# Decays' sums in one pass, reordered stage ends and a shared start in a nine-stage float32 network

## The chip, the cores and the metric

The kernel runs on one NeuronCore of a Trainium2 chip. The metric is the device time of one execution in microseconds; the time of a kernel is the median of its runs. Lines of the profile (L170) are lines of the kernel before. Its engines are called PE (TensorE's matmuls), PEld (its weight loads), DVE (VectorE), ACT (ScalarE), POOL (GpSimd) and SP (SyncE, which issues most transfers).

## The reference

256 tokens of width 1024, all in float32. A first block of two layers; each layer has a gated feed-forward network (hidden width 2816), a mixer, a cross attention to 256 memory tokens and a second feed-forward network, each between a norm before and a norm behind. Then a second block (a state-space branch and a dilated attention branch, mixed, then a third kind of feed-forward network) and a last norm. The change touches the start, the feed-forward networks' beginnings, the mixer and the norms. In the mixer half of the heads are a gated delta rule in both directions:

```
g = -exp(a_log) * softplus(a + dt_bias)          # per token, direction and head
g = cumsum(g)                                     # in each chunk
decay = exp(where(tril, g[i] - g[j], -inf))
lower = strict_lower((k*beta) @ k.T * decay)
sol   = triangular_solve(I + lower, [v*beta, k*beta*exp(g)])
qk    = (q @ k.T) * decay
...                                               # state from chunk to chunk
rms_norm(x, w) = x * rsqrt(mean(x*x) + 1e-6) * w
x = x + 0.5 * rms_norm(swiglu(rms_norm(x, pre)), post)
```

## The kernel before

Tokens are two tiles of 128 partitions. Each weight matrix comes in units of 128x1024 numbers (512 KB) through four raw buffers, on SP's queue; ACT rounds a unit to a high part (L148) and DVE subtracts for the low part (L149), in halves of 512 columns. Activations are split the same way behind a transposition (to_xT, L250; split, L175 and L177). Each product is then three matmuls, high by high, high by low, low by high (L170 to L172). An instruction stream per engine runs in its own order; a list scheduler sets that order from a model of times, except where issue_after holds an instruction behind another on its engine. The stages run one after the other: ffn1, mix, xat, ffn2, twice, then the second block and its ffn.

The start: sixteen matmuls of zeros (L1791), x of tile 0, the first norm's gain broadcast to 128 partitions, two units, x of tile 1, two units. set_pre multiplies x by the gain (L235) and take_pre transposes and splits it. In a feed-forward stage norms are deferred: the products are made from x times gain, and the norm's factor (rstd, computed by small operations, L189 to L193, after sums of squares on ACT, L205) comes in with the tanh (L364) and the products that follow (L365, L366). The first two blocks of 256 hidden columns are made by tokens (by_tokens: first tile 0 for both blocks, then tile 1, since tile 1's residual is still under way from the stage before: run_late); h is transposed (L371) and split. The other nine blocks are made by channels.

A stage ends with residual for each tile: the factor from the sums of squares on POOL (rstd with gpsimd), the product with the norm's gain (L296, L298), the update of x (L300), and set_pre for the next stage, with a second factor on POOL when the norm isn't deferred (L237).

In the mixer, strengths makes g, the prefix sums by a product with a triangle (L764), and decays(d) for a direction: for each of four heads, three times, a product whose stationary operand is one column of g, broadcast, and whose moving operand is the triangle (L805), so that all partitions hold the prefix sums as a row; masks are added by a product with the identity (L807); twelve exponentials on ACT follow. f32 products leave two records each in the trace; fp32r products one. In solve, four heads of two directions are solved with matmuls of 64 partitions and 64 columns in opposite quarters of the array (L1145, L1153), six phases a mixer. All this goes on beside fill, a stream of projections of which more(1) issues one step.

Rotary tables for the retention heads are made during the first feed-forward stage by its hook, which takes one step of a generator after each block by channels.

## Time and profile before

| what | value |
|---|---|
| median of 3 runs | 1946.12 us (1944.95 to 1948.43) |
| the profiled execution | 1947.42 us |
| its span, first to last instruction | 1945.2 us |
| mean granted TensorE clock | 0.998 |
| busy: PE, PEld, DVE, ACT, POOL | 1914.7, 1717.7, 1412.7, 1048.9, 185.7 us |
| matmul records | 12859 |
| read from HBM | 333.90 MB, 172 GB/s over the span |

The busy time of PE counts modelled ends of pipelined matmuls: what one matmul costs is read from the start of one to the start of the next. A row of the timeline may merge several instructions (x8).

### The profile page before, as it was taken

To read this page: it belongs to the slowest core of one execution; us is meant where nothing else is said; L and a number is where in the kernel's file an instruction comes from. 1 tells how busy PE (TensorE), PEld (TensorE's weight loads), DVE (VectorE), ACT (ScalarE), POOL (GpSimd) and SP (SyncE) were. 2 spreads that over 40 slices of the span, in tenths; PEclk is the share of its full clock that TensorE was granted. 3 is DMA by queue.
4 is the path that set the end of the run, shared out by engine and by line. 5 is a ranking of instruction groups with operands and counts; after the bars stand their busy time and mean duration, and the time that the engine had idled before them with its cause. 6 is when DMAs were issued, how large, how long until landed. Compare 5 with 4: busy or idle time off the path is not lost.

```text
span 1945.2 us, 34675 instructions
## 1 busy us (share of the span) xinstructions
PE 1914.7 (98%) x12859; PEld 1717.7 (88%) x12859; DVE 1412.7 (73%) x3002; ACT 1048.9 (54%) x2173; POOL 185.7 (10%) x407
## 2 busy tenths in 40 slices
PE   9999999999999999999999999999999999999998
PEld 6899888898899989999788978998999998888997
DVE  6777688775666766667987757666798988767765
ACT  5655465465554555546555645554555555546542
POOL 2000100020200110010100120002101111001000
PEclk9999999999999999999999999999999999999999
DMA  8666434364566556644434726655566646656651
GB/s 266 206 220 217 125 109 147 109 220 137 164 205 196 180 186 220 187 161 144 137 101 145 247 86 212 200 189 157 146 174 182 187 121 205 200 196 224 199 179 49
DMA packets 272887, 337.26 MB, mean 173 GB/s; under 512 B 19740, under 2 KB 223150, under 8 KB 272718
## 3 DMA queue, kind: packets, MB, share of 16 engines
q1 hardware_dynamic: 266980, 326.64, 53.6%
q10 hardware_dynamic: 5690, 8.25, 1.2%
q8 instruction: 101, 1.65, 0.3%
q14 instruction: 68, 0.56, 0.1%
q0 software_dynamic: 48, 0.16, 0.0%
HBM read 333.90 MB, written 1.08 MB: 172 GB/s over the span
## 4 chain that ended last, share of the span: by engine, by line
PE 84%; DVE 4%; POOL 3%; DMA 2%; ACT 2%; issue 2%; SPq 0%; ACTq 0%; POOLq 0%; DVEq 0%
PE bank L170 25%; PE bank L171 25%; PE bank L172 25%; DVE lo L149 2%; DMA raw<-in_ffn_up_dram 2%; PE bank L250 1%; POOL t L192 1%; POOL vh L213 1%; POOL y L193 1%; ACT hi L148 1%; PE bank L1003 1%; PE bank L1543 1%; ACT md L1034 1%; PE bank L1153 1%; PE bank L1256 1%
## 5 line engine op out<-in xcount | busy, mean ns | idle before, releaser
L148 ACT ACTIVATE hi<-raw 128x512 fp32r<-128x512 f32 (+1 forms) x1190 | 678.7, 615 | 413.6 <-PE bank L172 96.0
L149 DVE TENSOR_TENSOR lo<-raw,hi 128x512 fp32r<-128x512 f32 (+1 forms) x1190 | 764.7, 680 | 187.1 <-ACT hi L148 178.4
L170 PE MATMUL bank<-xh,hi 128*128 128x256 f32 x2080 | 588.8, 283 | 0.0
L171 PE MATMUL bank<-xl,hi 128*128 128x256 f32 x2080 | 585.1, 281 | 0.0
L172 PE MATMUL bank<-xh,lo 128*128 128x256 f32 x2080 | 584.7, 281 | 0.1
L170 PEld LDWEIGHTS bank<-xh,hi 128*128 128x128 f32 x2080 | 394.2, 190 | 4.1
L171 PEld LDWEIGHTS bank<-xl,hi 128*128 128x128 f32 x2080 | 393.9, 189 | 3.5
L172 PEld LDWEIGHTS bank<-xh,lo 128*128 128x128 f32 x2080 | 394.5, 190 | 0.6 <-DVE lo L149 0.6
L170 PE MATMUL bank<-hi,xh 128*128 128x512 f32 (+1 forms) x852 | 333.5, 392 | 3.5 <-ACT xh L175 2.2
L171 PE MATMUL bank<-lo,xh 128*128 128x512 f32 (+1 forms) x852 | 324.7, 381 | 5.2 <-DVE lo L149 5.1
L172 PE MATMUL bank<-hi,xl 128*128 128x512 f32 (+1 forms) x852 | 323.9, 380 | 0.5 <-DVE xl L177 0.5
L171 PEld LDWEIGHTS bank<-lo,xh 128*128 128x128 f32 x852 | 160.3, 188 | 34.8 <-DVE lo L149 9.9
L170 PEld LDWEIGHTS bank<-hi,xh 128*128 128x128 f32 x852 | 160.2, 188 | 31.5 <-ACT xh L175 3.5
L172 PEld LDWEIGHTS bank<-hi,xl 128*128 128x128 f32 x852 | 159.9, 188 | 28.8 <-DVE xl L177 2.2
L170 PE MATMUL bank<-hi,hh 128*128 128x512 f32 x440 | 175.9, 400 | 1.3 <-ACT hh L175 1.3
L171 PE MATMUL bank<-lo,hh 128*128 128x512 f32 x440 | 173.9, 395 | 0.0
L172 PE MATMUL bank<-hi,hl 128*128 128x512 f32 x440 | 173.4, 394 | 0.0
L213 POOL TENSOR_SCALAR vh<-ss 128x1 f32<-128x1 f32 x40 | 27.6, 689 | 1130.8 <-ACT junk L205 996.1
L402 ACT ACTIVATE th<-s 128x256 f32<-128x256 f32 x90 | 37.3, 414 | 124.3 <-DVE s L401 122.7
L172 PEld LDWEIGHTS bank<-hi,hl 128*128 128x128 f32 x440 | 82.7, 188 | 20.7 <-DVE hl L177 0.3
L170 PEld LDWEIGHTS bank<-hi,hh 128*128 128x128 f32 x440 | 82.7, 188 | 18.4 <-ACT hh L175 1.7
L171 PEld LDWEIGHTS bank<-lo,hh 128*128 128x128 f32 x440 | 82.7, 188 | 16.0
(369 smaller groups left out, 1991.4 us busy)
## 6 DMA issues: line engine op xcount, KB each, us to landing
raw<-in_w_in_dram SPq DMA_DIRECT2D x112, 512.0 KB, 4.4
raw<-in_ffn_gate_dram SPq DMA_DIRECT2D x176, 256.0 KB, 3.9
raw<-in_ffn_up_dram SPq DMA_DIRECT2D x176, 256.0 KB, 4.3
raw<-in_ffn_down_dram SPq DMA_DIRECT2D x88, 512.0 KB, 4.6
raw<-in_w_in_dram SPq DMA_DIRECT2D x96, 192.0 KB, 2.8
raw<-in_w_ffn_gate_dram SPq DMA_DIRECT2D x44, 256.0 KB, 3.8
raw<-in_w_ffn_up_dram SPq DMA_DIRECT2D x44, 256.0 KB, 4.1
raw<-in_w_ffn_down_dram SPq DMA_DIRECT2D x22, 512.0 KB, 4.6
```

Source lines behind the costliest of these rows:

```text
L148: nc.scalar.activation(hi[:, c], raw[:, c], AF.Copy)
L149: nc.vector.tensor_tensor(lo[:, c], raw[:, c], hi[:, c].bitcast(F32), ALU.subtract)
L170: mm(out, lhsT=lh, rhs=rh, start=start, stop=False)
L171: mm(out, lhsT=lh, rhs=rl, start=False, stop=False)
L172: mm(out, lhsT=ll, rhs=rh, start=False, stop=stop)
L192: V.tensor_scalar(t, y, y, vh, ALU.mult, ALU.mult)
L193: V.tensor_scalar(y, t, -1.5, y, ALU.add, ALU.mult)
L213: V.tensor_scalar(vh, s[:, 0:1], s[:, 1:2], 0.5 * EPS, ALU.add, ALU.add)
L250: self.nc.tensor.transpose(b[:, i * P:(i + 1) * P], src[:, (q + i) * P:(q + i + 1) * P], self.ident)
L402: last["A"] = nc.scalar.activation(th, s[:, 0], AF.Tanh)
L1003: T.matmul(b[:, j * 256:(j + 1) * 256], lhsT=lhs[:, h, j * P:(j + 1) * P], rhs=rhs[:, h], start=True, stop=True)
L1034: A.activation(md[r, :, :, :, s], mn[r, :, :, c0:c0 + 16].rearrange("p n h a -> p a h n"), AF.Copy, scale=self.half[s][r])
```

## The change

1. Decays: the prefix sums of each direction and tile are made once, as rows, on 36 partitions (32 to 35 repeat 0 to 3): g is copied to two places of a zeroed tile, four f32 products with the triangle make the rows, ACT rounds all 36 to fp32r, and DVE puts the residue on partitions 32 to 35. Then, for each head, one fp32r product with a 0/1 column (selr, broadcast) lays the sums of both directions and both tiles on all partitions, with both masks added, and a second one gives the unmasked far sums. decays is called with two heads for both directions in place of one direction for four heads. The chunk's total, once read off a row's end, is now a product with ones.
2. Solve: the matmuls of one phase are held in the order of (head, direction), each behind the one before.
3. Stage ends: residual's factor, and set_pre's when the norm isn't deferred, are computed on DVE; POOL keeps the deferred ones. In a feed-forward stage the update of x of tile 1 and its set_pre are held behind the tanh and the last product of the first block by tokens (self.behind).
4. First stage alone: the first two blocks by tokens alternate between the tiles after every two contraction steps, so that one unit serves both.
5. Start: the gain comes as eight rows of 128 and is transposed; x is transposed without it, and each 128-column split multiplies by its column. Unit 0 is loaded before tile 1 of x; twelve warm-up matmuls in place of sixteen.
6. Rotary tables for both tiles at once, with one sine, behind an added step of the generator.
7. Weight pools in the feed-forward stages by a fixed rule; the raw pool lies at the other side of the memory.

```
-        self.rawp = pool(ctx, "raw", 4)
+        self.rawp = ctx.enter_context(tc.tile_pool(name="raw", bufs=4, side="right", reuse_waits="tile"))
...
+            for i in range(m):
+                ix = (slice(None), k0 + q + i, slice(t * P, (t + 1) * P))
+                self.split(xT[0][ix], xT[1][ix], b[:, i * P:(i + 1) * P], cols[:, q + i:q + i + 1])
...
-        r = None if defer else self.rstd(self.halves(self.x[t]), D, pool)
-        xg = self.normed(self.x[t], g, r)
+        r = None if defer else self.rstd(self.halves(self.x[t]), D)
+        xg = self.x[t] if cols is not None else self.normed(self.x[t], g, r)
...
-            r = self.rstd(acc, D, self.nc.gpsimd)
+            r = self.rstd(acc, D)
...
+        with ExitStack() as es:
+            for ins in self.behind:
+                es.enter_context(self.tc.issue_after(ins))
+            if gpost is not None:
+                for xh, s in zip(self.halves(self.x[t]), self.halves(hg)):
+                    V.scalar_tensor_tensor(xh, s, r, xh, ALU.mult, ALU.add)
+            if gpre is not None:
+                self.set_pre(t, gpre, defer)
...
-                cnt[0] += 1
-                if j == 1 or kind == "dn" and (j > 6 or j == 0):
-                    return w2
-                return self.wp if j == 10 or cnt[0] % 3 == 0 else w2
+                if kind == "dn":
+                    return self.wp if 1 < j < 8 else w2
+                return self.wp if j == 10 or j in (8, 9) and q % 2 else w2
...
+            alone = self.late is None
+            if alone:
+                one, two = by_tokens_parts(0, 0), by_tokens_parts(1, 0)
+                next(one)
+                self.take_pre(1)
+                self.fence = self.last
+                for _ in range(3):
+                    next(two)
+                    next(one)
+                next(two)
...
+            else:
+                by_tokens(0, 0)
+                done = [last["A"].ins, last["V"].ins]
+                self.behind = done
+                self.run_late()
+                self.behind = []
+                by_tokens(0, 1, {4: flush, 6: lambda: self.take_pre(1)})
...
+                gg = w512()[:, :144].rearrange("p (t d c) -> p t d c", t=2, d=2)
+                V.memset(gg, 0.0)
+                for c in (0, 32):
+                    V.tensor_copy(gg[:, :, :, c:c + 4], g.rearrange("p t (d c) -> p t d c", d=2))
...
+                for d in range(2):
+                    T.matmul(pg[:, 16 + d * 4:20 + d * 4], lhsT=self.ones.to_broadcast([P, P]), rhs=g[:, d, d * 4:d * 4 + 4], start=True, stop=True)
+                    for n in range(2):
+                        t = n if d == 0 else 1 - n
+                        T.matmul(b[0:36, (2 * d + n) * P:(2 * d + n + 1) * P], lhsT=gg[:, t, d], rhs=self.tri[d], start=True, stop=True)
...
+                A.copy(gr[0:36], b[0:36])
+                V.tensor_tensor(gr[32:36], b[32:36], gr[32:36].bitcast(F32), ALU.subtract)
                 yield
-                decays(0)
+                decays((0, 1))
                 yield
-                decays(1)
+                decays((2, 3))
...
+                    sel = self.selr[:36, h:h + 1].to_broadcast([36, P])
+                    own, far = self.bank(), self.bank()
+                    T.matmul(own, lhsT=sel, rhs=gr[:36], start=True, stop=False)
+                    T.matmul(far[:, 0:256].rearrange("p (d c) -> p d c", d=2), lhsT=sel, rhs=gr[:36].rearrange("p (d t c) -> p d t c", d=2, t=2)[:, :, 1], start=True, stop=True)
+                    for d in range(2):
+                        T.matmul(own[:, d * 256:(d + 1) * 256].rearrange("p (t c) -> p t c", t=2), lhsT=self.identr, rhs=self.mskr[d].unsqueeze(1).to_broadcast([P, 2, P]), start=False, stop=d == 1)
...
+                turns = [(h, d) for h in range(4) for d in range(2)]
+                in_turn = lambda one: self.tc.issue_after(one.ins) if one else nullcontext()
...
+                        one = None
+                        for h, d in turns:
+                            with in_turn(one):
+                                one = T.matmul(bs[d][r[d], h * P:(h + 1) * P], lhsT=Z[d][r[d], h, n], rhs=rhs[d][r[d], h], start=True, stop=True)
...
+        yield
+        nc.scalar.activation(cs, ang, AF.Sin)
...
-        for _ in range(16):
+        for _ in range(12):
...
-    g0 = net.bcast(net.gp, pre_of(stages[0]), D, "gain", nc.sync)
+    g0 = net.gp.tile([P, D], F32, tag="gain", name="g0")
+    nc.sync.dma_start(g0[:8, :P], pre_of(stages[0]).rearrange("o (k p) -> (o k) p", p=P))
+    early = [units[0]()]
+    load_x(1)
+    net.stash = early + [u() for u in units[1:]]
```

## Rows read from the trace of the kernel before

**Rows 1.** The page, busy us of each engine (share of the span) and instructions:

```profile
PE 1914.7 (98%) x12859; PEld 1717.7 (88%) x12859; DVE 1412.7 (73%) x3002; ACT 1048.9 (54%) x2173; POOL 185.7 (10%) x407
```

**Rows 2.** What TensorE waited for: us in total, times, longest:

```profile
PE bank L171 <- DVE lo L149: 5.1, 7, 1.2
PE bank L371 <- DVE h L366: 4.7, 3, 1.7
PE bank L250 <- DVE xg L237: 2.7, 3, 1.3
...
PE bank L170 <- ACT hh L175: 1.3, 1, 1.3
```

**Rows 3.** Timeline of the start: start us, us, engine, instruction [idle before]:

```profile
4.06 1.61 PEld L1791 LDWEIGHTS <-zero 128*128 128x128 bf16 x8 [0.20 <-issue]
...
6.48 1.29 DVE L235 TENSOR_TENSOR xg<-x,gain 128x512 f32<-128x512 f32 x2 [5.37 <-DMA gain<-in_norm_pre_dram]
...
7.23 1.26 PE L250 MATMUL bank<-cst,xg 128*128 128x128 f32 x8 [1.07 <-DVE xg L235]
...
7.92 0.60 ACT L175 ACTIVATE xh<-bank 128x512 fp32r<-128x512 f32 x1 [2.41 <-PE bank L250]
...
8.71 1.15 ACT L148 ACTIVATE hi<-raw 128x512 fp32r<-128x512 f32 x2 [0.19 <-DMA raw<-in_ffn_up_dram]
...
9.39 0.50 PE L170 MATMUL bank<-hi,xh 128*128 128x512 f32 x1 [0.90 <-ACT hi L148]
...
17.00 0.40 PE L172 MATMUL bank<-hi,xl 128*128 128x512 f32 x1
17.23 0.39 PE L170 MATMUL bank<-hi,xh 128*128 128x512 f32 x1
```

**Rows 4.** Transfers issued in the first 30 us: KB each, us to landing:

```profile
gain<-in_norm_pre_dram SPq DMA_DIRECT2D x1, 512.0 KB
cst<-in_consts_dram POOLq DMA_DIRECT2D x1, 152.0 KB, 5.6
```

**Rows 5.** Busy time by stretch, 6 to 8 us (last number GB/s):

```profile
6.00:8.00 2.00, 0.93 (x6) 0.59 (x6) 1.29 (x2) 0.07 (x1) 1.68 (x4) 1.00 1.05 360
```

**Rows 6.** Groups by form, DVE and ACT: busy us, mean ns | idle before:

```profile
L192 DVE TENSOR_SCALAR t<-y,vh 128x1 f32<-128x1 f32 x30 | 8.1, 269 | 0.4
...
L177 DVE TENSOR_TENSOR al<-bank,ah 128x128 fp32r<-128x128 f32 x8 | 2.3, 287 | 1.8 <-ACT ah L175 1.8
...
L175 ACT ACTIVATE ah<-bank 128x128 fp32r<-128x128 f32 x8 | 2.1, 260 | 0.0
```

**Rows 7.** Timeline of TensorE, one direction's decays in the first mixer:

```profile
238.40 1.05 PE L805 MATMUL bank<-cst,g 128*128 128x128 f32 x8
239.21 0.47 PE L807 MATMUL bank<-mskr,identr 128*128 128x512 f32 x1
...
241.53 0.28 PE L170 MATMUL bank<-xh,hi 128*128 128x256 f32 x1
241.65 0.28 PE L171 MATMUL bank<-xl,hi 128*128 128x256 f32 x1
```

**Rows 8.** Timeline of TensorE, two phases of the solve, first mixer:

```profile
332.06 0.39 PE L172 MATMUL bank<-hi,xl 128*128 128x512 f32 x1
332.38 1.09 PE L1153 MATMUL bank<-ch,iv 64*64 64x128 f32 x16
...
338.69 1.08 PE L1145 MATMUL bank<-ch,M 64*64 64x128 f32 x8
...
342.20 1.08 PE L1145 MATMUL bank<-ch,M 64*64 64x128 f32 x8
```

**Rows 9.** Timeline of the entry into the second feed-forward stage:

```profile
494.56 1.42 DVE L300 SCALAR_TENSOR_TENSOR x<-hg,y,x 128x512 f32<-128x512 f32 x2 [4.32 <-POOL y L193]
...
498.27 0.44 PE L371 MATMUL bank<-cst,h 128*128 128x128 f32 x2 [1.66 <-DVE h L366]
```

**Rows 10.** Busy time by stretch, 520 to 600 us: PE, PEld, DVE, ACT, POOL:

```profile
520.00:600.00 80.00, 80.00 (x575) 75.11 (x574) 54.01 (x98) 41.07 (x80) 0.00 (x0) 1.00 0.64 202
```

More of the change, by code (lines that the diff above doesn't have):

```diff
@@ L1 @@
 import math
-from contextlib import ExitStack
+from contextlib import ExitStack, nullcontext
 import numpy as np
@@ L323, in ffn @@
             pend = []
-            cnt = [0]
             last = {}
@@ L348, in by_tokens, with by_tokens_parts @@
             def by_tokens(t, j, between={}):
+                for _ in by_tokens_parts(t, j, between):
+                    pass
+            def by_tokens_parts(t, j, between={}):
                 if j not in gu:
@@ L456, in ffn @@
                 if j == 2:
-                    DN(1, 0)
+                    if not alone:
+                        DN(1, 0)
                 elif j < 9:
@@ new lines, in rotary_tables @@
+        wk = self.nrm.tile([P, 512], F32, tag="junk", name="wk")
+        ang, k = (wk[:, c:c + 256].rearrange("p (t c) -> p t c", t=2) for c in (0, 256))
+        pi, pf = once[:, 0:2].bitcast(I32), once[:, 2:4]
+        nc.scalar.dma_start(pi, self.a["positions"][0].rearrange("(t p) -> p t", p=P))
+        V.tensor_copy(pf, pi)
+        cs = self.fp.tile([P, 2, P], F32, name="cs1")
+        for t in range(2):
+            V.tensor_scalar(ang[:, t, 64:128], once[:, C_FREQ - C_END:C_FREQ - C_END + 64], pf[:, t:t + 1], None, ALU.mult)
@@ L679, in mem_xT @@
+        c2 = float(np.array(int(c2), np.uint32).view(np.float32))
+        c3 = 2 * math.pi - c1 - c2
+        for c in (c1, c2, c3):
+            V.scalar_tensor_tensor(ang, k, -c, ang, ALU.mult, ALU.add)
+        V.tensor_scalar(ang[:, :, 0:64], ang[:, :, 0:64], math.pi / 2, None, ALU.add)
+        V.tensor_scalar(ang, ang, 3.1415925, -3.1415925, ALU.min, ALU.max)
+        yield
+        nc.scalar.activation(cs, ang, AF.Sin)
+        self.cs1 = [cs[:, t] for t in range(2)]
     def mem_xT(self, l):
@@ L1150, in solve @@
                         bs = [self.bank() for _ in range(2)]
-                        for h in range(4):
-                            for d in range(2):
-                                T.matmul(bs[d][r[d], h * P:(h + 1) * P], lhsT=Z[d][r[d], h, n], rhs=rhs[d][r[d], h], start=True, stop=True)
+                        one = None
+                        for h, d in turns:
+                            with in_turn(one):
+                                one = T.matmul(bs[d][r[d], h * P:(h + 1) * P], lhsT=Z[d][r[d], h, n], rhs=rhs[d][r[d], h], start=True, stop=True)
                         A.copy(y[0][r[0]], hd(bs[0])[r[0]])
```

143 lines of the change are left out of this document (65 added, 78 removed).

## The prediction

> **What bounds the kernel now.** I read the page first. TensorE is busy 1914.7 of 1945.2 us [rows 1]: the kernel is a stream of matmuls, and a change can win in two ways only, by taking matmul time out or by closing gaps between matmuls. The list of what TensorE waited for comes next [rows 2]. The reader is to see that its entries are few and each belongs to a place: the two L371 and L250 entries are the starts of stages, the L175 entry (hh) is one spot in the first feed-forward stage, the L171 entry (the residue of the weights' split) lies mostly in the two mixers and isn't touched here. Then the timeline of the places that the diff touches: the start [rows 3 to 5], the decays [rows 7], the solve [rows 8], the entry into a feed-forward stage [rows 9]. Away from these places TensorE has no gap: in 80 us of a feed-forward stage it is busy for 80.00, with DVE at 54.01 and ACT at 41.07 [rows 10].
>
> Times of the trace belong to an execution of 1947.42 us (span 1945.2); the median of the runs is 1946.12, so I take the sum from 1947.42 and 1.3 us off at the end.
>
> **The start.** Today the first product of weights begins at 9.39 us, and before it the gain's broadcast must land (6.48), the gain be multiplied in, the transposes run (7.23), and the first unit of weights land, split from 8.71 on [rows 3]. The broadcast moves 512 KB ahead of that unit in SP's queue [rows 4]; the DMA engines moved 360 GB/s in this stretch [rows 5], so its absence brings the first unit forward by about 1.5 us, to 7.2. The identity for the transposes comes with the constants on POOL's queue, 5.6 us after their issue [rows 4], which stands among POOL's first instructions: near 6.8, and the change doesn't move that. Transposes at 6.9, 0.7 us to the first split (7.23 to 7.92 today, by L250 and the split that follows it), a column split of some 0.26 on ACT and 0.29 on DVE in place of one of 512 columns [rows 6]: first product near 8.1, a gain of 1.3. Bounds: nothing, if the constants come later or ACT is taken by the weights' split; 2, if they come earlier.
>
> From there, 24 products of 512 columns take 9.39 to 17.23 = 7.84 us, while one follows the other in 0.23 when fed (17.00 to 17.23) [rows 3]: 5.5 us of work, so 2.3 lost to weights that aren't split yet. With both token tiles on each unit a unit feeds 12 products, 2.8 us, twice what it feeds now. I expect the 2.3 and some 0.5 behind it to shrink to 0.8, not to 0, because the sixteen column splits cost ACT 16 x 0.26 = 4.2 us in a place where it also splits weights. Gain 2.0 (bounds 1 and 2.8). Start together: **3.3** (1 to 4.8). The second tile's rows now come in SP's queue ahead of units 1 to 3; what is behind them is covered by those 2.8 us a unit.
>
> The warm-up loses four matmuls of 0.22 us (8 loads in 1.61 us from 4.06 on [rows 3]), and TensorE stands from about 5.3 to 6.9, where today it stands for 1.07. The spacing says that it rose from the 1.2 to the 2.4 GHz level near 4 us and kept it over the gap of today. The Trainium skill ("TensorE: Matmul & The Clock Gate", Part 1: The HAM clock gate) says that the throttled state is the default and that idleness brings it back; by it a longer gap could cost the level again. No row shows a gap of this length at the start, so this is a rival below, with the trace's own price.
>
> **Rotary tables.** One set of table operations on both tiles, one sine where there were two. They are DVE and ACT work under TensorE's stream. The one wait near it, 1.3 us for hh L175 [rows 2], falls where ACT does the second sine. It goes if no other ACT work takes its place; I take half: **0.7** (0 to 1.3). Its generator has one more step, so each later piece of the setup moves by one channel block; cover: the idle half of ACT in [rows 10].
>
> **Decays.** Today one direction takes from 238.40 to 241.53 = 3.13 us of TensorE: 24 records of 128 columns and two masks [rows 7]. Two directions, two mixers: 12.5. Added for each mixer and head: one product of 512 columns (0.23), one of 256 and two masks of 256 (0.12 each, 241.53 to 241.65 [rows 7]): 0.59, so 2.4 for four heads. Added once: two sums with a ones matrix and four products with the triangle, all f32, two records each, at the 0.10 of L805 (238.40 to 239.21 for eight): 12 records, 1.2. That makes 3.6, against 6.3. But 36 partitions are a shape that this trace doesn't have. The nearest row is the entry into the 64-row products of the solve, 332.06 to 332.38 = 0.32 after a matmul that otherwise takes 0.23 [rows 8]: 0.09 for the entry, taken again for the way back. Two switches a head: 0.7 a mixer. I take them: 6.3 - 3.6 - 0.7 = 2.0 a mixer, **4.0** in all (2.6 with twice that price, 5.4 with none). The Trainium skill ("TensorEngine Tiling (Array Packing)", Key Properties) says that changing the tiling mode drains TensorE; were 36 rows run in the 128-row mode the sum would be 5.4, and by the rule, with a change of mode, it is the 4.0. The copy and subtraction that split the sums, the memset and the copies are 6 small instructions on ACT and DVE, put one step of the products' stream ahead of their use; such a step holds 24 products of 0.12, about 3 us. If that cover were gone they would cost about 2 us a mixer. One buffer of the six of w512 is held longer; the convolutions use the others.
>
> **Solve.** The two directions use opposite quarters of the array. When their matmuls alternate, sixteen records are busy 1.09 us (332.38); when a direction runs alone, eight are busy 1.08 (338.69 and, apart from it, 342.20) [rows 8]. So a phase in two pieces costs twice. Going through the timeline of both mixers I count three of six phases in two pieces in each; the others alternate. The chain that forces the turns should save 1.0 us in each of the six split ones of the kernel: **6.0**. Upper bound 7.2, as each piece also pays an entry and a way back; lower bound 1.0, under the rivals.
>
> **Stage ends.** Into a feed-forward stage: POOL computes the factor of the second tile's residual, DVE sits 4.32 us for it, the update starts at 494.56, and the squares and gains that follow hold ACT and DVE ahead of the first block's tanh, so the transposes of h wait until 498.27 [rows 9]. This happens three times, 4.7 us in all [rows 2]. The change puts the updates behind the first block's tanh and products, and the factor on DVE, eight operations of at most 0.27 [rows 6], about 2 us. What is late next is the second tile's xT, needed only after the second block, 5.5 us of products on. **4.5** (3 to 5.2). Before cross attention (twice) and before the second block, both normalising factors go from POOL to DVE; the waits for xg L237 total 2.7 us [rows 2]. On DVE they queue behind splits of weights, so I take **2.0** (0.5 to 3).
>
> **At nothing:** the raw pool's other side, the fixed choice of weight pools, the split's type test. They add no instruction; [rows 10] is the cover of the pools: no gap with DVE and ACT a third or more idle.
>
> **Sum:** 3.3 + 0.7 + 4.0 + 6.0 + 4.5 + 2.0 = 20.5. 1947.4 - 20.5 = 1926.9 for an execution like the profiled one, **1925.6** as a median. With all lower bounds it is 1 + 0 + 2.6 + 1 + 3 + 0.5 = 8.1, a median of 1938.0; with all upper ones 4.8 + 1.3 + 5.4 + 7.2 + 5.2 + 3 = 26.9, 1919.2.
>
> **Rivals.** (1) The stage ends' stalls move instead of going: the small operations on DVE queue behind weight splits of 0.7 us each and the next products wait for those. For it: DVE is the next busiest engine [rows 1]. Against it: DVE sat idle for 4.32 us in just this place [rows 9]. Then 6.5 us aren't won: 1932.1.
> (2) The turns make TensorE wait: 338.69 to 342.20 leaves 2.5 us between the two pieces [rows 8], the two other split phases about 0.4 each; waited out in both mixers that is 6.6 us and eats the 6.0. For it: the second direction's rows come from DVE, which is behind ACT there. Against: other products stood in that gap and may stand ahead of the turns. 1925.6 + 6.6 = 1932.2.
> (3) The clock falls in the gap at the start. It had risen by 4.06 us of the span [rows 3]; the same stretch at the lower level costs at most half of it, 2.0 us: 1927.6. Against it: the level held over the gap of 1.07. The rule of the Trainium skill cited at the start ("TensorE: Matmul & The Clock Gate", Part 1) is what this case would come from.
> (4) Slower: the weight pools. Gates and ups now take nearly all of their tiles from one pool of eight, so the next block's four units wait for the block before the last to be released. If those units come late, all 45 channel blocks of the five feed-forward stages pay; from 0.55 us each this outweighs everything above (45 x 0.55 = 24.7 against 20.5), and at 1 us the time is 1970.6. Against it: a block lasts some 17 us (96 products of 0.12, 24 of 0.23), and the splits of four units need 8 x 0.7, under 6, of DVE, which has 26 in 80 free [rows 10].
> (5) Nothing is left: the new order opens as many gaps, of the kind of L171 [rows 2], as it closes; within 0.2%, which is about what a measurement of this kernel can tell from no change.
>
> **How the numbers follow.** The sum as it stands 0.56, (1) 0.20, (2) 0.09, (3) 0.04, (4) 0.06, (5) 0.05. Faster by over 0.2% (under 1942.2) is the first four, 0.89; same 0.05; slower 0.06. The range goes from just under the upper bounds' 1919.2 to beyond (1) and (2), 1918 to 1936; outside lie (4), (5) and a part of the likeliest's own low end.
>
> **What would show it.** Start: the first L170 at 8 us and 48 products in under 12.5. Decays: one stretch of L805's successors near 2.2 us for two heads. Solve: six groups of sixteen records a mixer. Stage ends: no wait of L371 for h, DVE instead of POOL in L189 to L193. The prediction is wrong if the list of TensorE's waits has new entries above 2 us in the feed-forward stages or in the solve, or if the products' busy time falls by less than 7 us while the gaps remain.

## The result, and the profile after

The changed kernel takes 1975.92 us (median of 4 runs, 1973.75 to 1976.78), the kernel before 1945.78 beside it: ratio 1.0151 (95% interval 1.0139 to 1.0164), 30 us slower where 20.5 us less were forecast. The profiled execution has a span of 1974.3 us against 1945.2 and a mean granted clock of 0.986 against 0.998.

The page's busy times after (us, share of the span, instructions; [rows 1] before):

```profile
PE 1924.9 (97%) x12808; PEld 1726.8 (87%) x12808; DVE 1454.5 (74%) x3215; ACT 1049.0 (53%) x2186; POOL 108.5 (5%) x199
```

What TensorE waited for after (us, times, longest; [rows 2] before). Line numbers have moved: L152 is the weights' low part, L254 the transposition, L824 the four products that make the rows of sums, L869 a head's product, L1140 the last 32x32 products of the inverse, L388 the transposition of h.

```profile
PE bank L254 <- DVE xg L240: 11.5, 7, 2.6
PE bank L824 <- DVE w L815: 9.1, 2, 4.6
PE bank L1140 <- issue: 6.1, 2, 3.4
PE bank L174 <- DVE lo L152: 4.6, 4, 1.4
PE bank L869 <- DVE gr L829: 2.8, 2, 1.4
PE bank L173 <- ACT xh L178: 2.0, 1, 2.0
PE bank L254 <- DVE xg L238: 1.9, 1, 1.9
```

The waits of L371 for h are gone, as forecast. Three entries stand above 6 us, none of which the prediction had as a cost: L824 in the decays (with L869 behind it, 2.8), L1140 in the inverse, and a larger L254 at the stage ends.

I lined up the same products in both traces and took the difference of their starts (after less before); a stretch's share is the growth of that difference:

| stretch (us in the trace before) | first layer | second layer |
|---|---|---|
| all up to the mixer (0 to 218) | +1.6 | |
| feed-forward stages between the mixers (526 to 884) | | +1.5 |
| decays: from the prefix sums to the sums of k (235 to 256; 901 to 922) | +8.7 | +9.6 |
| inverse: 32x32 products (307 to 322; 974 to 988) | +6.6 | +4.4 |
| solve (322 to 364; 988 to 1030) | -2.0 | -2.0 |
| mixer's end to the first scores (376 to 436; 1042 to 1102) | +3.8 | +1.5 |
| cross attention and entry into ffn2 (436 to 526; 1102 to 1194) | -4.1 | -5.6 |
| end of the last ffn2, entry to the second block (1194 to 1361) | | +6.1 |

With what lies between (-1.0) that is the span's 29.1. The first row hides two parts: at 175 us the changed kernel is 3.9 us ahead, and up to 218 it loses 5.4, behind waits of 2.5 us in all for xg and lo and a stretch at half clock. The timeline of the first mixer's decays after, all engines but the weight loads:

```profile
244.54 0.18 DVE L813 MEMSET w<- 128x144 f32 x1
244.76 0.25 DVE L815 COPY w<-g 128x16 f32<-128x16 f32 x2
245.15 1.89 PE L824 MATMUL bank<-cst,w 128*36 128x128 f32 x8 [4.57 <-DVE w L815]
...
247.08 0.58 ACT L828 CAST gr<-bank 36x512 fp32r<-36x512 f32 x1
...
247.70 0.68 DVE L829 TENSOR_TENSOR gr<-bank,gr 4x512 fp32r<-4x512 f32 x1 [1.68 <-ACT gr L828]
...
248.43 0.79 PE L869 MATMUL bank<-gr,selr 36*128 36x512 f32 x1 [1.39 <-DVE gr L829]
```

The reader is to see the order on DVE: g had been ready since 231.85, but the zeroing of gg starts at 244.54, behind a convolution's operations, since gg lies in the ring of six w512 buffers that the convolutions use. TensorE waits 4.57 us, then 1.39 for the split of the sums. Behind it the granted clock is half (by stretch: PE, PEld, DVE, ACT, POOL, then the clock; [rows 7] ran at 1.00):

```profile
240.00:245.00 5.00, 0.58 (x5) 0.38 (x4) 4.89 (x13) 1.86 (x4) 0.00 (x0) 0.95 0.47 136
245.00:255.00 10.00, 8.46 (x33) 6.76 (x34) 5.24 (x11) 6.07 (x17) 0.00 (x0) 0.52 0.10 37
255.00:265.00 10.00, 10.00 (x60) 8.47 (x59) 6.15 (x12) 7.79 (x21) 0.00 (x0) 1.00 0.19 54
```

Such stretches at 0.5 (the 1.2 GHz level) follow eight waits of the changed kernel: 8.9 to 12.4, 179.6 to 183.0, 244.5 to 254.7, 326.4 to 333.2, 435.6 to 439.0, 923.7 to 937.4, 1009.0 to 1012.5 and 1374.3 to 1377.7 us, 48 us in all. Before there is none between 4 us and the last 20.

The inverse, timeline of TensorE after; then the instruction queue in 323 to 330 us (packets, MB, share):

```profile
323.12 1.28 PE L1140 MATMUL bank<-zd,f 32*32 32x32 f32 x124
327.81 0.32 PE L1140 MATMUL bank<-zd,f 32*32 32x32 f32 x4 [3.42 <-issue]
```

```profile
q8 instruction: 2, 0.03, 1.7%
```

TensorE stops 3.42 us four matmuls short of the end, and no semaphore is named: it waited for nothing that its data need.

The first mixer's stage end after, timeline of DVE and the product that waits for it:

```profile
426.70 0.26 DVE L195 TENSOR_SCALAR t<-y,vh 128x1 f32<-128x1 f32 x1
426.88 0.68 DVE L305 TENSOR_TENSOR hg<-bank,gain 128x512 f32<-128x512 f32 x1
427.48 0.20 DVE L196 TENSOR_SCALAR y<-t,y 128x1 f32<-128x1 f32 x1
427.60 0.68 DVE L180 TENSOR_TENSOR xl<-bank,xh 128x512 fp32r<-128x512 f32 x1
428.19 0.27 DVE L195 TENSOR_SCALAR t<-y,vh 128x1 f32<-128x1 f32 x1
...
433.69 1.41 DVE L240 SCALAR_TENSOR_TENSOR xg<-x,y,gain 128x512 f32<-128x512 f32 x2
...
434.49 1.51 PE L254 MATMUL bank<-cst,xg 128*128 128x128 f32 x8 [2.03 <-DVE xg L240]
```

Each of the factor's small operations is followed by another one's operation of 0.68 us: the chain is one instruction long at a time, and xg comes 2 us late.

### The profile page after: what moved, and what is told of

Read it like the earlier page. It is cut to its first block, busy times and chain, and to the rows that moved or that the text cites. A ratio compares the mean times of both kernels' runs of the same rounds, so it can differ in the third digit from the quotient of the medians.

```text
span 1974.3 us, 34506 instructions
## 1 busy us (share of the span) xinstructions
PE 1924.9 (97%) x12808; PEld 1726.8 (87%) x12808; DVE 1454.5 (74%) x3215; ACT 1049.0 (53%) x2186; POOL 108.5 (5%) x199
## 3 DMA queue, kind: packets, MB, share of 16 engines
HBM read 333.38 MB, written 1.08 MB: 169 GB/s over the span
## 4 chain that ended last, share of the span: by engine, by line
PE 88%; DVE 6%; ACT 3%; DMA 2%; issue 1%; POOL 0%; SPq 0%; ACTq 0%; DVEq 0%
PE bank L173 26%; PE bank L175 26%; PE bank L174 25%; DVE lo L152 2%; PE bank L254 1%; ACT junk L208 1%; PE bank L1064 1%; ACT hi L151 1%; PE bank L1298 1%; PE bank L1321 1%; PE bank L1608 1%; ACT md L1095 1%; PE bank L1232 1%; PE bank L1218 0%; DVE t L195 0%
## 5 line engine op out<-in xcount | busy, mean ns | idle before, releaser
L152 DVE TENSOR_TENSOR lo<-raw,hi 128x512 fp32r<-128x512 f32 (+1 forms) x1190 | 767.6, 681 | 186.0 <-ACT hi L151 178.0
L173 PEld LDWEIGHTS bank<-xh,hi 128*128 128x128 f32 x2080 | 399.0, 192 | 5.2 <-ACT hi L151 0.4
L174 PEld LDWEIGHTS bank<-xl,hi 128*128 128x128 f32 x2080 | 399.2, 192 | 3.3
L175 PEld LDWEIGHTS bank<-xh,lo 128*128 128x128 f32 x2080 | 399.0, 192 | 2.0 <-DVE lo L152 1.3
L418 DVE TENSOR_TENSOR s<-bank,rows 128x512 f32<-128x512 f32 x90 | 61.8, 687 | 88.3 <-PE bank L175 63.3
```

The costliest lines, as they stand in the source:

```text
L152: nc.vector.tensor_tensor(lo[:, c], raw[:, c], hi[:, c].bitcast(F32), ALU.subtract)
L173: mm(out, lhsT=lh, rhs=rh, start=start, stop=False)
L174: mm(out, lhsT=lh, rhs=rl, start=False, stop=False)
L175: mm(out, lhsT=ll, rhs=rh, start=False, stop=stop)
L418: nc.vector.tensor_tensor(s, bb, rows[0], ALU.mult)
```

## The experiments

Theory: four separate losses, namely the decays' order on DVE, a stall of instruction loading in the inverse, the factors on DVE, and something at the entry to the second block; half-clock stretches behind the longest waits enlarge each. Rivals are in the expectations. "Against before" is (ratio - 1) x 1946 us; the intervals of the ratios are about 0.0015 wide to each side (3 us), 0.001 in some, so finer shares are read from the traces, each a single execution. A trace can hold a stretch at half clock that another one with the same instructions in that place lacks, worth some 2 us, so the clock of a place is read before a difference is put down to an edit.

| run | median, us | ratio (95% interval) | against before | span, us |
|---|---|---|---|---|
| changed | 1975.92 | 1.0151 (1.0139 to 1.0164) | +29.4 | 1974.3 |
| own_gg | 1975.04 | 1.0150 (1.0135 to 1.0165) | +29.2 | 1971.0 |
| fill | 1959.66 | 1.0070 (1.0052 to 1.0088) | +13.6 | 1958.0 |
| late | 1955.64 | 1.0044 (1.0029 to 1.0059) | +8.6 | 1953.1 |
| old_decays | 1949.98 | 1.0020 (1.0010 to 1.0031) | +3.9 | 1946.0 |
| shift | 1965.69 | 1.0099 (1.0084 to 1.0114) | +19.3 | 1963.7 |
| pool_rstd | 1974.03 | 1.0145 (1.0129 to 1.0160) | +28.2 | 1972.4 |
| old_pools | 1962.90 | 1.0080 (1.0063 to 1.0096) | +15.6 | 1964.5 |
| turns | 1941.85 | 0.9977 (0.9968 to 0.9987) | -4.5 | 1942.7 |
| turns_behind | 1936.14 | 0.9941 (0.9924 to 0.9957) | -11.5 | 1935.5 |
| start | 1936.15 | 0.9946 (0.9931 to 0.9960) | -10.5 | 1934.8 |
| start_alt | 1935.98 | 0.9943 (0.9928 to 0.9958) | -11.1 | 1934.4 |
| rot | 1935.58 | 0.9943 (0.9928 to 0.9958) | -11.1 | 1936.6 |
| raw_side | 1938.03 | 0.9953 (0.9938 to 0.9968) | -9.1 | 1936.2 |
| wpools | 1947.05 | 1.0005 (0.9995 to 1.0014) | +1.0 | 1946.3 |
| dve_rstd | 1940.31 | 0.9963 (0.9949 to 0.9977) | -7.2 | 1939.0 |
| decays_late | 1943.71 | 0.9979 (0.9969 to 0.9989) | -4.1 | 1941.5 |
| kept | 1932.47 | 0.9922 (0.9909 to 0.9934) | -15.2 | 1929.4 |
| best | 1933.64 | 0.9931 (0.9918 to 0.9945) | -13.4 | 1931.4 |

**own_gg** (the changed kernel, gg out of the ring):

```
-                gg = w512()[:, :144].rearrange("p (t d c) -> p t d c", t=2, d=2)
+                gg = S("gg", 144).rearrange("p (t d c) -> p t d c", t=2, d=2)
```

> The changed kernel with the zeroed tile gg in a buffer of its own, not in the ring of six w512 buffers. Theory 1 (in the changed kernel TensorE waits 4.7 us a mixer at L824 because the ring's buffer comes free late, so that the memset and copies stand behind the convolutions on DVE; the granted clock falls to half behind that wait): both waits and the low clock at 244 to 255 and 924 to 937 go, 16 to 18 us less, 1958 to 1961 us. Theory 2 (the new products on 36 partitions are dear themselves, wherever they stand): the wait goes but less than 5 us is won, 1971 us or more.

Neither theory as I put it. The wait at L824 is gone and a longer one stands behind it; timeline of own_gg, ACT, DVE and PE:

```profile
246.45 0.63 ACT L665 ACTIVATE th<-acc 128x512 f32<-128x512 f32 x1 [2.36 <-DVE acc L664]
246.98 0.56 ACT L828 CAST gr<-bank 36x512 fp32r<-36x512 f32 x1
...
247.83 0.68 DVE L829 TENSOR_TENSOR gr<-bank,gr 4x512 fp32r<-4x512 f32 x1
...
248.57 0.79 PE L869 MATMUL bank<-gr,selr 36*128 36x512 f32 x1 [5.91 <-DVE gr L829]
```

The products of the sums were through by 239.5, but ACT's rounding stands behind a convolution's tanh, which waits for DVE. The wait moved one link down the same chain: 4.57 and 1.39 became 5.91.

**fill** (own_gg, with constants multiplied where TensorE waits):

```
+                    if h == 0:
+                        for _ in range(26):
+                            T.matmul(own, lhsT=self.tri[0].bitcast(bf)[:, :P], rhs=self.cst[:, 0:256].bitcast(bf), start=True, stop=True)
```

> The changed kernel with gg in a buffer of its own and 26 products of constants (bf16, 512 columns, overwritten by what follows) ahead of the first head's product, in the place where TensorE waits 6.1 us a mixer for the split sums. Read in the stretch of the decays alone, since later TensorE instructions shift. Theory (a wait of TensorE brings the granted clock to half for a while behind it, and that is some 4 us a mixer of the loss): with the wait filled the clock stays at full, and the decays' stretch costs 3 to 5 us a mixer less although nothing comes earlier. Rival (the low clock belongs to the products on 36 partitions or to what else is done there): the clock falls as before, and the stretch takes the same time or more.

Busy time and clock by stretch, own_gg first, then fill:

```profile
242.00:248.00 6.00, 0.66 (x6) 0.45 (x4) 3.90 (x8) 3.06 (x7) 0.00 (x0) 0.99 0.57 173
248.00:258.00 10.00, 9.43 (x50) 8.33 (x51) 6.36 (x12) 6.35 (x17) 0.00 (x0) 0.66 0.00 1
```

```profile
242.00:248.00 6.00, 5.93 (x31) 2.99 (x31) 3.81 (x8) 2.96 (x7) 0.00 (x0) 1.00 0.55 171
248.00:258.00 10.00, 9.71 (x65) 7.94 (x64) 7.34 (x14) 7.88 (x23) 0.00 (x0) 1.00 0.14 41
```

The first head's product starts at 248.67, no earlier than own_gg's 248.57, and the clock stays at 1.00. The decays' stretch grows by 5.3 us a mixer instead of 8.0 and 8.5 (own_gg): the half clock is worth 2.6 and 3.2 us there. The theory holds. (The rest of this run's gain is the inverse's stall, which its 52 more records, 26 products and their loads, shifted away; see shift.)

**late** (own_gg, decays two steps later):

```
-  *qkv(1, {0: s}), *qkv(2, {0: s, 1: s, 3: s}), tokens(512, "rk", {3: lambda: turn("rk")}),
+  *qkv(1, {0: s}), *qkv(2, {0: s, 3: s}), tokens(512, "rk", {1: s, 3: lambda: turn("rk")}),
```

> The changed kernel with gg in a buffer of its own and the heads' products of the decays two steps of the products' stream later (they follow the split of the sums by three steps of some 2.9 us in place of one). Theory 1 (what costs 18 us in the decays is only the wait for the split sums, 6.1 us a mixer with gg alone moved, since ACT's rounding and DVE's subtraction stand behind the convolutions, and the half clock behind it): waits at L869 under 1 us, no low clock there, the decays' stretch at or below its time before; 18 to 20 us less than the changed kernel, 1955 to 1958. Theory 2 (the split follows the products wherever they are put, as the convolutions of the later steps hold ACT and DVE in the same way): a wait of 3 us or more stays, 1965 or more.

Theory 1: waits of 0.60 us are left at L869 (0.76 from start to start), and the stretch grows by 0.0 us in each mixer. Unhindered, one mixer's new decays (L821, L824, L869, L870, L872, from start to next start) take 0.61 + 1.11 + 1.32 + 0.82 + 1.56 = 5.42 us, the old ones 6.27 (L805 5.02, L807 1.25). But the clock does fall, just behind the stretch: from 260.2 to 263.7 and from 929.3 to 932.7 us it is at half. Timeline of TensorE:

```profile
248.90 0.46 PE L869 MATMUL bank<-gr,selr 36*128 36x512 f32 x1 [0.60 <-DVE gr L829]
...
258.13 1.84 PE L888 MATMUL bank<-ones,xg 128*128 128x1 f32 x16
...
261.35 0.63 PE L174 MATMUL bank<-lo,xh 128*128 128x512 f32 x1
261.77 0.63 PE L175 MATMUL bank<-hi,xl 128*128 128x512 f32 x1
```

Products of 512 columns start every 0.43 us there in place of 0.23, eight of them, and that is the 1.5 us a mixer by which all that follows is late. The expectation of decays_late puts these 1.5 us down to later exponentials; the trace shows no wait for them here.

**old_decays** (the changed kernel with strengths and decays as before):

> The changed kernel with strengths and decays of the kernel before, all else as changed. By both theories of the decays their 18 us come back: 1958 us. TensorE has fewer instructions in each mixer, so that its blocks of 256 instructions fall otherwise: if the stall of 3.4 and 2.7 us inside the 32x32 products (L1140) is instruction loading, it moves or goes too, up to 11 us more, 1947 us; if it is a wait for data, it stays where it is and the time is 1956 to 1960.

Both: 1950, the decays' 18 us are back and the stall at L1140 is gone as well.

**shift** (the changed kernel, 64 more TensorE instructions at the start):

```
+        for _ in range(32):
+            nc.tensor.matmul(b[:, :8], lhsT=zero[:, :P], rhs=zero[:, :8], start=True, stop=True)
```

> The changed kernel with 32 more tiny products of zeros (8 columns) behind the warm-up, so that all later TensorE instructions stand 64 places later in their blocks of 256. Theory (the stall inside L1140 is TensorE's instruction loading): the stall leaves L1140 in both mixers and the low clock behind it goes; 8 to 11 us less, 1965 to 1968 us, unless the new place of the loads is a quick stretch too. Rival (a wait for data): it stays at L1140 with 3.4 and 2.7 us, and the time within 2 us of 1976.

The theory, with 10 us won. Timeline of shift, the same products:

```profile
323.60 1.31 PE L1140 MATMUL bank<-zd,f 32*32 32x32 f32 x128
```

The 256 records of this stretch pass in 1.1 us. I counted TensorE's records (PE and PEld, with the semaphore and drain records among them, from 0) in blocks of 256; start to start of the longest gap inside the stretch, all at place 193 of a block, and in all six runs ahead of the same two records, 4289 and 13505:

| run | place of the stretch's first record, mixers 1 and 2 | gap, us |
|---|---|---|
| changed | 200, 196 | 3.6, 2.9 |
| own_gg | 200, 196 | 2.0, 2.9 |
| pool_rstd | 200, 196 | 2.2, 2.9 |
| old_pools | 200, 196 | 2.8, 3.5 |
| decays_late | 206, 201 | 1.2, 0.5 |
| late | 199, 194 | 0.7, 0.8 |
| shift | 8, 4 | none |
| before, and twelve other runs | 246 to 255, 32 to 42 | none (under 0.07) |

**pool_rstd** (the changed kernel, factors on GpSimd):

```
-            r = self.rstd(acc, D)
+            r = self.rstd(acc, D, self.nc.gpsimd)
```

(and the same in set_pre)

> The changed kernel with the factors of residual and of set_pre on GpSimd again, as before; the order behind the first block kept. Theory (on DVE the eight small operations interleave with weight splits of 0.68 us, so that xg comes late at six stage ends and the clock falls behind the longest waits): the waits of L254 for xg L240 fall from 11.5 us to under 4, 8 to 13 us less, 1963 to 1968 us. Rival (the late xg comes from the order of the stage ends, not from the engine): within 3 us of 1976.

A miss: only 1 to 2 us, though the waits for xg fall from 11.5 to 4.3 us as forecast: others take their place. The first mixer's end loses nothing any more (+3.8 became 0), but a wait of the cross attention behind it, which the late xg had covered, is back (+2.4 in place of -2.1), and the entry to the second block still loses 4.7 us. So something else is late there.

**turns** and **turns_behind** (the kernel before with the chain of turns; then also with self.behind, factors on GpSimd):

```
+            self.behind = done
             self.run_late()
+            self.behind = []
```

> The kernel before with the chain of turns in the solve alone. By the drift of the changed kernel 2.0 us a mixer are won in this stretch: 3.9 us less than before, 1942 to 1943 us. My sum had 6.0 for it, 1940. The rival of the prediction (TensorE waits out the turns): no change.

> The kernel before with the turns and with the updates of x and set_pre behind the first block's tanh and products (self.behind), the factors left on GpSimd. If the order is what takes the waits of L371 away: 4 to 5 us less than with the turns alone, 1937 to 1939 us. If the factors on DVE were needed for it, or the second tile's x now comes late instead: the same as with the turns alone or more.

Turns: 3.9 us in the two solves by the trace, as the drift said (its span is only 2.5 shorter, since a wait of 1.96 us for hh, 1.28 before, and the half clock behind it, 88.0 to 91.4 us, take 2.2 back). Solve's split phases after (timeline of the changed kernel; [rows 8] before):

```profile
355.48 0.43 PE L1209 MATMUL bank<-ch,M 64*64 64x128 f32 x2
358.56 1.08 PE L1209 MATMUL bank<-ch,M 64*64 64x128 f32 x14
```

A pair goes first and the other fourteen follow: 0.43 + 1.08 in place of 1.08 + 1.08, 0.65 for each of six split phases. Turns and order together: the waits of L371 for h are gone without the factors on DVE.

**wpools** (turns_behind with the fixed rule for the weight pools and the raw pool's other side) and **raw_side** (the side alone):

> The kernel before with the turns, the order behind the first block, and the fixed rule for the weight pools with the raw pool at the other side (all else as before). Theory (the rule leaves other weight tiles free where a stage ends, so that splits of the next stage's units stand on DVE ahead of xg; the changed kernel loses 6 us at the entry to the second block, and 4.7 still with the factors on GpSimd): 3 to 6 us more than turns_behind, 1939 to 1942, lost at the ends of stages. My rival 4 (the blocks of a feed-forward stage wait for weights): a drift that grows along the stages, 1960 or more. My own step (nothing): 1936.

> The kernel before with the turns, the order behind the first block, and the raw pool at the other side of the memory (with its own way of waiting for reuse); the weight pools' rule as before. Theory (the rule is the cost: it makes a block's units wait for the block before the last, so that transfers and splits run some 20 us later at the end of a stage): as turns_behind, 1936. Rival (the raw pool's placing or its waits delay the transfers): 1944 to 1947.

The rule is the cost, 10.8 us by the spans (12.5 by the ratios); the side alone, with its way of waiting for reuse, is 0.7 by the spans (2.3 by the ratios, within their intervals). SyncE's issues at the end of the last ffn2, turns_behind first, then wpools:

```profile
1282.47 0.37 SPq L145 DMA_DIRECT2D raw<-in_ffn_gate_dram  x1
...
1283.46 18.47 SPq L145 DMA_DIRECT2D raw<-in_ffn_down_dram  x6
1303.64 20.83 SPq L145 DMA_DIRECT2D raw<-in_w_in_dram  x16
```

```profile
1301.36 0.37 SPq L145 DMA_DIRECT2D raw<-in_ffn_gate_dram  x1
...
1309.89 10.69 SPq L145 DMA_DIRECT2D raw<-in_ffn_down_dram  x6
1321.46 24.77 SPq L145 DMA_DIRECT2D raw<-in_w_in_dram  x16
```

wpools is some 5 us behind by then, so of the 18.9, 26.4 and 17.8 us between the issues some 12 to 21 are lost lead: transfers and splits run that much closer to their use. In the blocks here it costs nothing (1194 to 1318 us of before: 0.7 us less, if anything). At the end it does: the next block's units (w_in) are split while the stage ends (ACT and DVE of wpools):

```profile
1335.61 0.63 ACT L150 ACTIVATE xh<-raw 128x512 fp32r<-128x512 f32 x1 [1.91 <-DMA raw<-in_w_in_dram]
...
1336.60 1.02 DVE L151 TENSOR_TENSOR lo<-raw,hi 128x384 fp32r<-128x384 f32 x2
1337.54 0.68 DVE L151 TENSOR_TENSOR xl<-raw,xh 128x512 fp32r<-128x512 f32 x1
```

In turns_behind the last such split before the stage end is over by 1323.5. The entry to the second block costs 5.2 us by this. The rest is 2.0 at the entry to the second layer, 2.3 in the second cross attention (with a stretch at half clock, 1123.7 to 1127.1) and 2.0 in the first feed-forward stage, less small gains between. In that stage one block does lose: TensorE waits 1.71 us for hh at 104.19, since a split for whose transfer ACT waited 2.17 us stands ahead of the tanh.

**old_pools** (the changed kernel with the old rule and side):

> The changed kernel with weight pools and raw pool as before. If the 10.9 us that they cost on the kernel before stand in the changed kernel as well: 1963 to 1967, with the waits for xg at the entry to the second block down from 5.4 to under 3 us; the decays' and the 32x32 products' losses stay, if their places among the instructions do. Rival (with the factors on DVE and the waits of the mixers the lead of the weights no longer matters): 1973 or more.

As the theory: 14 us less by the ratios (9.8 by the spans), although the decays' and L1140's losses stay; the waits for xg at the entry to the second block go from 5.1 to 2.6 us. In the trace 4.2 us of it come near 180 us already, ahead of the first mixer, where the changed kernel's waits and half clock are gone.

**dve_rstd** (turns_behind, factors on DVE):

> The kernel before with the turns, the order behind the first block, and the factors of residual and set_pre on DVE. Theory (the chain of eight small operations is cut by weight splits of 0.68 us, xg comes later): 4 to 9 us more than turns_behind, 1940 to 1945, at the two ends of the mixers, the entry to the second block and the entry to the feed-forward stage behind the second block's layers; the clock falls at some of these. The step of my prediction (2.0 us won at the ends of mixers): 1934.

The theory at its lower end: 3.5 us lost by the trace, 4.3 by the ratios. The mixers' ends lose 3.5 and 3.8 us and the cross attentions behind them win part of it back. The clock falls at 417.6, 1079.8 and 1352.9.

**start** and **start_alt** (turns_behind with the whole start, or with the alternation alone):

> The kernel before with the turns, the order behind the first block, and the whole new start: gain by columns, unit 0 ahead of tile 1 of x, twelve warm-up products, alternate tiles. By the drift of the changed kernel 1.0 to 1.6 us are lost up to the end of the first two blocks: 1937 to 1938. My sum had 3.3 us won: 1933.

> The same, but of the start only the alternation of the two tiles in the first two blocks; gain, loads and warm-up as before. Theory (the alternation saves what I put on it, 2.0 us, and the columns of the gain lose it again, as ACT must split x in sixteen pieces behind the squares and the weights): 1934, so about 3 us less than with the whole start. Rival (the second tile's x comes too late for the alternation, which waits for it): 1937 or more.

No difference in either that these medians show. In the traces the 96th of the first products starts at 36.02 before, 34.59 in the changed kernel, 33.80 in start_alt and 35.97 in start: the alternation wins 2.2 us there, and the rest of the new start gives 0.8 to 2.2 of it back. The clock is part of both: start runs at half from 9.1 to 15.9 us, and start_alt from 84.0 to 87.4, behind a wait of 1.80 us for hh, and there loses 1.9 of its 2.2 again. So these two runs are no fair price of their edits; kept and best are nearer to one. My own reading of a loss of 1.2 us at 48 us was an error: an output product stands earlier in the new order.

**rot** (turns_behind with the rotary tables): no difference.

> The kernel before with the turns, the order behind the first block, and the rotary tables for both tiles at once with the added step. The wait of 1.8 us for hh near 84 us goes (my sum had 0.7 won, bounds 0 and 1.3). Theory from the changed kernel (the added step moves the memory tokens' norm by one block, so that xg is late near 176 us, 1.2 and 1.1 us of waits and a stretch at half the clock): 2.3 us lost against 1.8 won, 1936 to 1938. Without that: 1934 to 1935.

1.1 us are won up to the first mixer, and 2.2 lost behind it, 1.6 of them where the clock is at half from 458.0 to 461.4 us, behind a wait of 1.39 us for xh. turns_behind has the same wait in the same place at full clock, so this loss can't be put down to the tables.

**decays_late** (turns_behind with the new decays, own buffer, two steps later):

> The kernel before with the turns, the order behind the first block, and the new decays with gg in a buffer of its own and the heads' products two steps later. By the records of TensorE the new decays take 12.45 us against 14.17 in both mixers, where they don't wait: 1.7 us less, and 0.76 us a mixer of wait stay if ACT and DVE are as full as with the rule: 1935 to 1936 us. If the weights' lead shortens that wait: 1934. Rival (the second step's exponentials and the later use of E push the pairs back by 1.5 us a mixer, as in the late run): 1938 to 1939.

More than the rival's: 6.0 us lost by the trace, but not by the rival's mechanism. Waits of 0.46 and 0.60 us at the heads, a stretch at half clock in each mixer (255.6 to 262.5 and 921.2 to 928.1), gaps of 1.2 and 0.5 us at L1140. Over each of the two stretches the difference to turns_behind grows by 3.15 us, 6.3 in all: without the half clock this run would be about even with turns_behind, by that estimate. So the new decays don't pay here even when their operands are early enough, and nearly all of what they lose is the clock.

**kept** (the changed kernel with decays, weight pools, raw pool and the factors' engine as before) and **best** (turns_behind, alternation, tables):

> The changed kernel with the decays, the weight and raw pools and the engine of the factors as before: turns, order behind the first block, new start, alternate tiles and rotary tables stay. If the three parts account for the loss: the 9.6 us that turns and order won alone, nothing for the start, up to 1 for the rotary tables: 1935 to 1937 us (ratio 0.994). If something else in the changed kernel loses as well: 1939 or more.

> The kernel before with turns, order behind the first block, alternate tiles in the first two blocks with the start otherwise as before, and the rotary tables. If the drifts of the runs alone add (start_alt up to the first mixer 0.35 us ahead of turns_behind, rot 1.06): 1934 to 1935 us. If a wait won in one place comes back in another: 1936, as turns_behind.

kept beats both kernels, by more than expected: the start and the tables together win 3.5 us up to the first mixer, where start and rot alone won about 1 each and start_alt 0.3. The traces show why: neither kept nor best falls to half clock up to there, though kept waits 2.35 us ahead of its first product, and without the wait for hh near 85 us nothing takes the alternation's gain back. kept's page and its longest waits:

```profile
PE 1905.8 (99%) x12856; PEld 1713.7 (89%) x12856; DVE 1411.0 (73%) x2999; ACT 1050.3 (54%) x2184; POOL 182.3 (9%) x407
```

```profile
PE bank L173 <- ACT xh L178: 5.2, 6, 2.4
PE bank L174 <- DVE lo L152: 4.2, 4, 1.2
PE bank L254 <- DVE xg L240: 2.7, 3, 1.3
```

## Why the prediction was wrong

Three steps of the sum failed: the weight pools at nothing, the cover of the decays' small operations, and the sign of the factors on DVE. A fourth loss, the stall in the inverse, stood in no step.

**At nothing.** This step failed outright. I named as cover that no block had a gap; the rule spent the stream's lead, and the lead is used where a stage ends. My rival 4 had the right mechanism and mostly the wrong place: it asked for 0.55 us in each of 45 blocks; one block of the first stage lost 1.9 us, the others nothing to speak of, and the ends and entries of stages most of the 10.8.

**Decays.** Forecast 4.0 won. The matmuls' term was 2.0 a mixer and measures 0.85: heads 0.92 us each in place of 0.77 (the masks 0.20 each, not 0.12; the 36-row product 0.33, the 0.32 that I took), the once-made products 1.7 in place of 1.2. The Trainium skill ("TensorEngine Tiling (Array Packing)", Key Properties) has a drain at a change of mode; 0.33 against 0.23 agrees, on 36 rows. The failed step is the cover: "put one step of the products' stream ahead of their use" holds for the program, not for in-order engines full of convolutions; I put 2 us a mixer on its loss, and it was 6 us of wait and some 3 of half clock. The half clock stood in the prediction at the start alone, as rival 3.

**What no step had.** The decays also changed how many TensorE instructions stand before the inverse, 10 us in the changed kernel (shift). The Trainium skill ("Runtime: NRT & Kernel Launch", Instruction fetch mechanics) has instructions come in blocks of 256, the crossing mostly hidden. The trace fits the count (the two records that wait, 4289 and 13505, lie 36 times 256 apart, though 512 or 1024 would fit them too) and shows an exception to the second: where 256 records pass in 1.1 us, and the stretch began 1 to 13 places behind place 193, the next turn of that place waited 0.5 to 3.6 us. That place 193 is where the load must have landed is my reading; no row shows the request.

**Stage ends.** The entries into feed-forward stages were right (4.5; by the order alone 5.2 at the three entries, turns_behind against turns; the 7.2 between their spans hold 2.3 of the half clock near 88 us in turns). The 2.0 us for the factors on DVE had the wrong sign: rival 1, with its mechanism as written, costs 3.5.

**Solve.** Right mechanism, 3.9 for 6.0: the term for a split phase was 1.0 and measures 0.65, since the pieces became 2 and 14, not one. Rival 2 did not come.

**Start and tables.** 3.3 and 0.7 forecast. The start wins 1.4 us at the 96th product, and 1.6 at 60 us by the products' starts; with the tables the changed kernel is 3.2 us ahead at 100 us, so here the sum was near. The first product is at 9.21, not 8.1: in ACT's order (timeline after) unit 0's split and the squares go ahead of the columns.

```profile
7.14 1.15 ACT L151 ACTIVATE hi<-raw 128x512 fp32r<-128x512 f32 x2 [0.71 <-DMA raw<-in_ffn_up_dram]
...
8.19 0.61 ACT L208 ACTIVATE junk<-x 128x512 f32<-128x512 f32 x1
...
8.81 0.35 ACT L178 ACTIVATE xh<-bank,g 128x128 fp32r<-128x128 f32 x1
...
9.21 0.79 PE L173 MATMUL bank<-hi,xh 128*128 128x512 f32 x1 [1.96 <-ACT xh L178]
```

Rival 3 came true in the changed kernel (half clock from 8.9 to 12.4, behind a wait of 1.96 us) and in five more traces with the new start, but not in late, shift, old_decays and kept, whose start is the same (shift's has the small products besides); wpools has it with the old start. Its price can be read where the starts are alike, at 60 us against before: late, shift, old_decays and kept are 1.4 to 1.6 us ahead at full clock, the changed kernel 1.6, pool_rstd, fill and old_pools 1.3, 1.0 and 0.3, and own_gg and start, at half clock for 6.8 us, 0.3 and 0.1. So it cost nothing that shows in the changed kernel and at most 1.5 us elsewhere, where the rival had 2.0. The tables win 1.0 to 1.7 us between 60 and 100 us in the traces of the changed kernel, kept, best and rot, where the medians can't tell 0.7 from nothing.

**Sum.** By spans, kept is 15.8 us faster than before and the changed kernel 29.1 slower: decays, rule and engine cost 44.9 together. By themselves: 28.3 (changed less old_decays, the shifted instructions in it), 10.8 (wpools less turns_behind), 3.5 (dve_rstd). The other 2.3 us are not attributed. By the ratios it is 44.6 together, and 25.5, 12.5 and 4.3 by themselves. What kept keeps stood in the forecast at 14.5 (3.3, 0.7, 6.0 and 4.5) and wins 15.8; its parts measure 3.5 up to the first mixer, 3.9 in the solves and 5.2 at the entries, 12.6, and the other 3.2 are not placed, so the agreement is partly luck. Why the clock also falls in late and decays_late behind waits of 0.46 to 0.60 us stays open.

## What to carry to other kernels

An edit that adds no instruction can still spend a stream's lead: look for the stage's end, where the next stage's first transfers and splits must already be over. For small operations on an in-order engine, cover is what stands ahead of them on that engine, not what the consumer does meanwhile; and moving the first of a chain's waits shows the next. Before a stretch of very short instructions, compare its place among the instruction blocks in both kernels before calling a change slow. Look at the granted clock in each stretch before you name the cause of a difference: the 1.5 us a mixer that one expectation here put down to late exponentials was the clock.

## What the runs showed of the hardware that was not expected

- TensorE can stop where no semaphore holds it: up to 3.6 us inside 256 records that otherwise take 1.1 us, or nothing, by where the stretch begins in a block of 256. That the place decides is shown (shift); that it waits for its own instructions is what fits, not shown.
- A single wait brought the half clock with it: 3.4 us at 0.5 behind the wait of 2.03 us at 432 us, 10.2 and 13.7 us behind the two of 4.6. In the kernel before, whose longest listed wait is 1.9 us, it never fell in the middle. The length of a wait doesn't decide alone: a wait of 1.39 us near 456 us brought the fall in rot and the same one none in turns_behind, kept's 2.35 us at the start brought none, and in late it fell behind 0.60 us, right behind sixteen products of one column. The Trainium skill ("TensorE: Matmul & The Clock Gate", Part 1) has idleness bring the lower level back; fill agrees, the clock at 1.00 with the same stretch kept busy.
